# When the splits of the weights are given to the scheduler: at the first unit, or three half chunks ahead

## The chip, the cores and the metric

The kernel runs on one core of one Trainium2 chip. The metric is the device time of one execution in microseconds (us), the median of several runs. Engines: TensorE (PE; its weight loads are PEld), VectorE (DVE), ScalarE (ACT), GpSimd (POOL) and SyncE (SP), which here only issues loads.

## The reference

One decoder layer for 256 tokens of width 2048, in float32. Three token mixers read the same normalised input, their outputs are gated and merged, and a gated MLP follows. Cut to what matters:

```python
h = rmsnorm(x, norm_attn[l])
(q_n, kc_n, ..., q_h, f_h, i_h, g_h, gates) = jnp.split(h @ w_in[l], split_at, axis=-1)
o_nsa = nsa_mixer(...)        # compressed, selected and sliding-window attention
o_sb = stick_breaking(q_s, k_s, v_s)
o_hg = hgrn2(q_h, f_h, i_h, g_h, lb_all[l], hg_norm_gain[l])   # gated linear recurrence
y = jnp.einsum('btnc,ncd->btnd', jnp.stack([o_nsa, o_sb, o_hg], axis=2), w_branch[l])
x = x + jnp.sum(gsig * y, axis=2) @ w_out[l]
x = x + conv_ffn(rmsnorm(x, norm_ffn[l]), w_up[l], conv_w[l], conv_b[l], w_down[l])
```

Some 313 MB, nearly all of it weights, go through the load queue, each weight once for 256 tokens.

## The kernel before

The weights stream in as **chunks** of 128x2048 float32 (1 MB, a tile `raw`, three buffers), loaded on SP's queue. Each chunk is worked on as two **halves** of 128x1024. A half has to be **split** before TensorE can use it: ScalarE rounds it to a high part `whi` (a CAST, L291) and VectorE subtracts to get the low part `wlo` (L292). `whi` and `wlo` have three buffers each, so the split of half h can start when TensorE is done with half h-3. A half feeds 16 or 12 matmuls. There are 593 halves, numbered here from 0 in the order of their use.

The work is a list of **units** (`plan`), in order: first recurrence group, second recurrence group, two stick-breaking groups, gates and branch products, the sparse-attention projections, more gates and branch products, the output projection, the MLP up (44 units) and down. `run` takes units from the list; `unit_b`, `unit_b2`, `unit_a` and `unit_g` call `half` (or `split_to`) for each half they need. The token mixers' own work (`hgrn`, `stick`, `nsa_keys`, `nsa`) is written as generators; after each half `pump` lets the first generator write its next piece, so mixer work stands between the units' matmuls.

A scheduler then sets each engine's order. Of the instructions that it reckons ready, it takes the one that was written first; each engine runs its list strictly in that order. So the place in which a split is *written* decides whether it goes ahead of mixer work that is ready at the same time.

`split_to(n)` (L82) writes splits until n halves are done, and `half` (L127) calls it with the present half plus 1 and then plus `ahead` = 3. In `split_to` the name `n` is also set inside the loop, to the width of a piece:

```python
while self.nsplit < min(n, 2 * len(self.src)):
    ...
    n = 1024 if self.nsplit else 512
```

So after the first pass the loop's bound is 512 and then 1024, beyond the number of halves: the first call writes the loads and the splits of all weights, ahead of everything that the units and mixers write later.

Lines that the prediction names: L184/L185 and L227 to L229 are the units' matmuls, with high and low parts. L234/L235 add up the two sums of a finished `unit_b` (ScalarE, VectorE); L780 (GpSimd) or L782 (VectorE) then scales the result. L436/L437 end `hgrn`; L318 is a scan in the second group's `hgrn`. L502/L503, L504 (Ln) and L508 (Exp) are in `rstd_feat`, and with L517 and L523 they make `norm_feat`, which normalises four query tiles of the sparse attention; L649 makes 16 matmuls of scores from them. L805 is a sigmoid on the gates. Ln, Exp and sigmoid each have an ACT_TABLE_LOAD ahead of them where ScalarE's function changes. `keep_warm` (L210) writes 11 matmuls at the start that only keep TensorE busy.

Of the kernel before, what the change touches and what calls it, by code (L numbers as in the profile page):

```python
# [45 lines left out]
class Net:  # L46
# [35 lines left out]
    def split_to(self, n):  # L82

        nc = self.nc
        while self.nsplit < min(n, 2 * len(self.src)):
            i, j = divmod(self.nsplit, 2)
            self.load_to(i + 1)
            if self.src[i].shape[1] < 2048:
                if not j:
                    self.parts[self.nsplit] = self.split_gate(self.raw[i])  # L90
                self.nsplit += 1
                continue
            raw = self.raw[i][:, 1024 * j:1024 * (j + 1)]
            hi = self.wp.tile([P, 1024], F32R, name="whi", bufs=3)
            lo = self.wp.tile([P, 1024], F32R, name="wlo", bufs=3)
            n = 1024 if self.nsplit else 512
            for c in range(0, 1024, n):
                self.splits.append(self.parts_of(raw[:, c:c + n], hi[:, c:c + n], lo[:, c:c + n]))
                self.casts.append(self.cast)
            self.parts[self.nsplit] = (hi, lo)  # L100
            self.nsplit += 1
# [1038 lines left out]
```

## Time and profile before

| | us |
|---|---|
| median of 3 runs | 1755.03 |
| the runs | 1753.78 to 1756.65 |
| the profiled execution | 1755.64 |
| its span, first to last instruction | 1753.9 |
| TensorE busy | 1744.5 (99%) |
| VectorE busy | 1111.6 (63%) |
| ScalarE busy | 949.4 (54%) |
| GpSimd busy | 127.4 (7%) |

A busy time is the union of an engine's instructions; matmuls overlap, so two that follow each other at 0.23 us each show 0.39 us of length. An instruction's start is therefore the safer mark than its end. Mixer stages run from the start to about 900 us, the MLP from about 1036 us on.

### The profile page before, as it was taken

How to read it: one execution, taken by the hardware profiler on the slowest of the kernel's cores; microseconds unless marked ns; L12 is line 12 of the kernel's file. 1: busy time of each engine (PE TensorE's matmuls, PEld its weight loads, DVE VectorE, ACT ScalarE, POOL GpSimd, SP SyncE). 2: the span in 40 equal slices, each digit the busy share in tenths (PEclk: the TensorE clock that was granted, in tenths of full speed). 3: DMA queues.
4: the chain of work that ended last, by engine and by line, in shares of the span. 5: the costliest groups of instructions: out<-in, count | busy, mean ns of one | idle time of the engine just before them, and what ended most of it. 6: DMA issues, size and time to landing. Idle time of an engine off the chain costs nothing.

```text
span 1753.9 us, 22831 instructions
## 1 busy us (share of the span) xinstructions
PE 1744.5 (99%) x9095; PEld 1487.4 (85%) x9095; DVE 1111.6 (63%) x1421; ACT 949.4 (54%) x1236; POOL 127.4 (7%) x114
## 2 busy tenths in 40 slices
PE   9999999999999999999999999999999999999999
PEld 7888888888888888888888888888888888888887
DVE  6588686756457555765566567777777777644443
ACT  7464745665445575555544565555555555533332
POOL 1110000000001000100011001111111001000000
PEclk9999999999999999999999999999999999999999
DMA  7544443545556444444456555555555555555663
GB/s 285 188 176 162 148 169 144 193 167 179 195 189 253 161 181 168 168 163 152 165 177 231 192 177 187 192 190 192 192 192 192 189 186 188 192 202 200 209 206 109
DMA packets 47835, 324.53 MB, mean 185 GB/s; under 512 B 5440, under 2 KB 5952, under 8 KB 9968
## 3 DMA queue, kind: packets, MB, share of 16 engines
q1 hardware_dynamic: 44784, 313.47, 50.3%
q0 software_dynamic: 1792, 7.50, 1.1%
q10 hardware_dynamic: 1152, 2.10, 0.3%
q8 instruction: 71, 1.16, 0.3%
q14 instruction: 36, 0.29, 0.0%
HBM read 320.96 MB, written 2.10 MB: 184 GB/s over the span
## 4 chain that ended last, share of the span: by engine, by line
PE 98%; ACT 1%; DVE 1%; DMA 0%; issue 0%; SPq 0%; DVEq 0%
PE acc L184 30%; PE acc L185 16%; PE acc L227 11%; PE acc L229 11%; PE acc L228 11%; PE mx L227 5%; PE mx L229 5%; PE mx L228 5%; PE mx L410 1%; PE mx L712 1%; PE mx L680 1%; PE mx L594 0%; DMA raw<-wb_in 0%; PE mx L831 0%; ACT whi L291 0%; PE mx L700 0%
## 5 line engine op out<-in xcount | busy, mean ns | idle before, releaser
L292 DVE TENSOR_TENSOR wlo<-raw,whi 128x1024 fp32r<-128x1024 f32 (+1 forms) x593 | 744.1, 1255 | 528.3 <-ACT whi L291 527.2
L291 ACT CAST whi<-raw 128x1024 fp32r<-128x1024 f32 (+1 forms) x594 | 622.3, 1048 | 667.4 <-PE acc L229 274.1
L184 PE MATMUL acc<-xs,whi 128*128 128x512 f32 x2304 | 808.2, 394 | 1.9 <-ACT whi L291 1.9
L185 PE MATMUL acc<-xs,wlo 128*128 128x256 f32 x2304 | 649.3, 282 | 1.3 <-DVE wlo L292 1.3
L184 PEld LDWEIGHTS acc<-xs,whi 128*128 128x128 f32 x2304 | 433.1, 188 | 97.7 <-ACT whi L291 3.1
L185 PEld LDWEIGHTS acc<-xs,wlo 128*128 128x128 f32 x2304 | 436.2, 189 | 3.7 <-DVE wlo L292 2.8
L227 PE MATMUL acc<-whi,xs 128*128 128x512 f32 x672 | 266.2, 396 | 0.1
L229 PE MATMUL acc<-whi,xs 128*128 128x512 f32 x672 | 262.0, 390 | 0.0
L228 PE MATMUL acc<-wlo,xs 128*128 128x512 f32 x672 | 261.6, 389 | 0.0
L229 PEld LDWEIGHTS acc<-whi,xs 128*128 128x128 f32 x672 | 126.1, 188 | 27.1
L227 PEld LDWEIGHTS acc<-whi,xs 128*128 128x128 f32 x672 | 126.3, 188 | 25.3 <-issue 0.2
L228 PEld LDWEIGHTS acc<-wlo,xs 128*128 128x128 f32 x672 | 126.3, 188 | 25.0 <-issue 0.2
L228 PE MATMUL mx<-wlo,act 128*128 128x512 f32 x352 | 136.9, 389 | 0.0
L227 PE MATMUL mx<-whi,act 128*128 128x512 f32 x352 | 136.9, 389 | 0.0
L229 PE MATMUL mx<-whi,act 128*128 128x512 f32 x352 | 136.9, 389 | 0.0
L1028 POOL TENSOR_TENSOR u<-u,rb 128x512 f32<-128x512 f32 x44 | 52.5, 1192 | 524.0 <-DVE u L235 524.0
L229 PEld LDWEIGHTS mx<-whi,act 128*128 128x128 f32 x352 | 66.1, 188 | 13.8
L228 PEld LDWEIGHTS mx<-wlo,act 128*128 128x128 f32 x352 | 66.1, 188 | 13.7
L227 PEld LDWEIGHTS mx<-whi,act 128*128 128x128 f32 x352 | 66.1, 188 | 13.6
L780 POOL TENSOR_TENSOR b<-b,rb 128x512 f32<-128x512 f32 x24 | 36.7, 1532 | 543.7 <-DVE b L235 489.6
L227 PE MATMUL acc<-whi,bo 128*128 128x512 f32 x192 | 75.7, 394 | 0.0
L229 PE MATMUL acc<-whi,bo 128*128 128x512 f32 x192 | 74.9, 390 | 0.0
(251 smaller groups left out, 1247.9 us busy)
## 6 DMA issues: line engine op xcount, KB each, us to landing
raw<-wb_up SPq DMA_DIRECT2D x88, 1024.0 KB, 4.8
raw<-wa_in SPq DMA_DIRECT2D x68, 1024.0 KB, 4.8
raw<-wb_in SPq DMA_DIRECT2D x53, 1024.0 KB, 4.8
raw<-wa_dn SPq DMA_DIRECT2D x44, 1024.0 KB, 4.8
raw<-wa_br SPq DMA_DIRECT2D x24, 1024.0 KB, 4.8
raw<-wa_out SPq DMA_DIRECT2D x16, 1024.0 KB, 4.8
b<-cw POOLq DMA_DIRECT2D x8, 512.0 KB, 4.8
raw<-wb_in SPq DMA_DIRECT2D x5, 512.0 KB, 9.2
```

Of the source, the lines that this page charges most:

```text
L184: mm(ps[:, j], hi[:, n], x(kt, slice(0, 2), al), start=kt == 0, stop=False)
L185: self.tail = mm(ps[:, j, T:], lo[:, n], x(kt, 0, al), start=False, stop=kt == KT - 1)
L227: mm(ps[tt], x(kt, 0, s), hi[:, k], start=kt == 0, stop=False)
L228: mm(ps[tt], x(kt, 0, s), lo[:, k], start=False, stop=False)
L229: mm(ps[tt], x(kt, 1, s), hi[:, k], start=False, stop=kt == 4 * n - 1)
L291: self.cast = self.nc.scalar.copy(hi, x)
L292: return self.nc.vector.tensor_tensor(lo, x, hi.bitcast(F32), op=ALU.subtract)
L410: mm(ps[:, h, blk], ke[:, 2 * pr + h, t], qe[:, 2 * pr + h, t], start=True, stop=True)
L680: mm(ps, q[g][:, hl, tt * P:(tt + 1) * P], kk[:, g::2, :w], start=True, stop=True)
L712: mm(po[h][:, tq], vv[:, kb, (2 * u + g) * P:(2 * u + g + 1) * P], pT[:, i], start=False, stop=i == n - 1)
L780: net.scaled(lambda: nc.gpsimd.tensor_tensor(d, d, rb2, op=ALU.mult))
L1028: nc.gpsimd.tensor_tensor(u[:, :, 2:], u[:, :, 2:], rb2, op=ALU.mult)
```

## The change

The width of a piece gets a name of its own, so the loop's bound stays the argument. The splits (and the loads with them) are then written by each call only as far as it asks: three halves ahead of the half in use. No instruction is added or taken away.

```diff
@@ split_to
-            n = 1024 if self.nsplit else 512
-            for c in range(0, 1024, n):
-                self.splits.append(self.parts_of(raw[:, c:c + n], hi[:, c:c + n], lo[:, c:c + n]))
+            w = 1024 if self.nsplit else 512
+            for c in range(0, 1024, w):
+                self.splits.append(self.parts_of(raw[:, c:c + w], hi[:, c:c + w], lo[:, c:c + w]))
```

What moves is the order on TensorE, VectorE and ScalarE. GpSimd's and SP's lists stay as they were, so no load changes its place. Counted by the number of splits that stand ahead of it, 721 of VectorE's 827 other instructions and 520 of ScalarE's 610 keep their place; most others move by one split, and on TensorE 20 of 546 mixer instructions move. Three places follow.

**The norm of the queries (`norm_feat` in `nsa`), ScalarE, about 647 us.** Before, from the last of three casts of weights on (t_7175 to t_7181 are the four tiles of sums, b_7255 a gate):

```order
L504 ACTIVATE t_7177<-mx,eps 128x512
L291 CAST nh<-t_7179 128x512
L291 CAST whi<-raw 128x1024
L291 CAST nh<-t_7181 128x512
L504 ACTIVATE t_7179<-mx,eps 128x512
L805 ACT_TABLE_LOAD
L805 ACTIVATE b_7255<-acc,rcol 128x512
L291 CAST whi<-raw 128x1024
L504 ACT_TABLE_LOAD
L504 ACTIVATE t_7181<-mx,eps 128x512
L291 CAST whi<-raw 128x1024
L508 ACT_TABLE_LOAD
```

Casts of weights stand between the norm's instructions here. Now, in the same place (t_5253 to t_5259 are the same four tiles):

```order
L291 CAST whi<-raw 128x1024 x3
L504 ACT_TABLE_LOAD
L504 ACTIVATE t_5253<-mx,eps 128x512
L504 ACTIVATE t_5255<-mx,eps 128x512
L291 CAST nh<-t_5257 128x512
L805 ACT_TABLE_LOAD
L805 ACTIVATE b_5347<-acc,rcol 128x512
L504 ACT_TABLE_LOAD
L504 ACTIVATE t_5257<-mx,eps 128x512
L291 CAST nh<-t_5259 128x512
L805 ACT_TABLE_LOAD
L805 ACTIVATE b_5347<-acc,rcol 128x512
```

and directly behind these, on the same engine:

```order
L504 ACT_TABLE_LOAD
L504 ACTIVATE t_5259<-mx,eps 128x512
L508 ACT_TABLE_LOAD
L508 ACTIVATE t_5253<-t_5253 128x512
L508 ACTIVATE t_5255<-t_5255 128x512
L508 ACTIVATE t_5257<-t_5257 128x512
L508 ACTIVATE t_5259<-t_5259 128x512
L291 CAST whi<-raw 128x1024 x4
```

Eighteen instructions now stand between two casts of weights (those of halves 210 and 211) where at most four stood.

**The scores, TensorE, same place.** Before, the first seven of the 16 score matmuls stand behind half 212 and the other nine five to seven halves later; now all stand around the first matmul of half 211:

```order
L502 MATMUL mx<-nh,onesr 128x512
L227 MATMUL acc<-whi,bo 128x512
L228 MATMUL acc<-wlo,bo 128x512
L503 MATMUL mx<-nh,onesr 128x512
L229 MATMUL acc<-whi,bo 128x512
L649 MATMUL mx<-kcmp,b_4771 128x15 x4
L649 MATMUL mx<-kcmp,b_5008 128x15 x2
L227 MATMUL acc<-whi,bo 128x512
L649 MATMUL mx<-kcmp,b_5008 128x15 x2
L649 MATMUL mx<-kcmp,b_4771 128x15 x4
L649 MATMUL mx<-kcmp,b_5008 128x15 x4
L228 MATMUL acc<-wlo,bo 128x512
```

They moved ahead by 23 to 107 of the units' matmuls, and L503 with them stands nearer to half 211.

**The end of the first `hgrn`, VectorE, about 196 us**, while the second group's last unit runs. Before (t_4227 and t_4256 are the two results):

```order
L436 TENSOR_TENSOR t_4227<-t_4227,b_3608 128x512
L437 SCALAR_TENSOR_TENSOR t_4227<-mx,sc,t_4227 128x512
L292 TENSOR_TENSOR wlo<-raw,whi 128x1024
L235 TENSOR_TENSOR b_4324<-acc,b_4324 128x512
L292 TENSOR_TENSOR bo<-t_4227,bo 128x2x256
L292 TENSOR_TENSOR wlo<-raw,whi 128x1024
```

and now (t_1552, t_1587):

```order
L436 TENSOR_TENSOR t_1552<-t_1552,b_793 128x512
L436 TENSOR_TENSOR t_1587<-t_1587,b_793 128x512
L235 TENSOR_TENSOR b_1669<-acc,b_1669 128x512
L437 SCALAR_TENSOR_TENSOR t_1552<-mx,sc,t_1552 128x512
L292 TENSOR_TENSOR wlo<-raw,whi 128x1024
L292 TENSOR_TENSOR bo<-t_1552,bo 128x2x256
```

The low part of half 62 has moved behind the second L436 and behind L235. At the end of the second `hgrn` (half 94) the same stands, with L782 ahead of the low part as well.

## Rows read from the trace of the kernel before

**Rows 1.** The page, part 2: granted TensorE clock in 40 slices.

```profile
PEclk9999999999999999999999999999999999999999
```

**Rows 2.** Waits of TensorE: engine, line, releaser: us in total, times, longest us.

```profile
PE acc L184 <- ACT whi L291: 1.9, 2, 1.0
PE acc L185 <- DVE wlo L292: 1.3, 3, 0.6
PE mx L649 <- DVE b L523: 0.9, 1, 0.9
```

**Rows 3.** Windows: stretch, busy us of five engines (x), granted clock, DMA share, GB/s.

```profile
10.00:12.00 2.00, 0.98 (x4) 0.30 (x2) 1.08 (x2) 1.59 (x3) 0.00 (x0) 1.00 1.00 412
12.00:14.00 2.00, 1.47 (x6) 1.31 (x6) 2.00 (x5) 2.00 (x4) 0.00 (x0) 0.69 1.03 420
14.00:16.00 2.00, 2.00 (x8) 1.65 (x7) 1.95 (x3) 1.88 (x4) 0.00 (x0) 0.50 1.04 426
16.00:18.00 2.00, 2.00 (x13) 1.78 (x12) 2.00 (x6) 2.00 (x5) 0.00 (x0) 0.96 1.03 406
```

**Rows 4.** Timeline of ScalarE at the norm: start, us, instruction, idle before and releaser.

```profile
647.38 1.05 ACT L291 CAST whi<-raw 128x1024 fp32r<-128x1024 f32 x1 [1.66 <-PE acc L229]
648.44 1.28 ACT L504 ACT_TABLE_LOAD   x1
649.74 1.27 ACT L504 ACTIVATE t<-mx,eps 128x512 f32<-128x512 f32 x2
650.89 0.62 ACT L291 CAST nh<-t 128x512 fp32r<-128x512 f32 x1
651.41 1.05 ACT L291 CAST whi<-raw 128x1024 fp32r<-128x1024 f32 x1
654.88 0.69 ACT L805 ACTIVATE b<-acc,rcol 128x512 f32<-128x512 f32 x1
660.76 1.15 ACT L508 ACTIVATE t<-t 128x512 f32<-128x512 f32 x2
```

**Rows 5.** Timeline of TensorE at the norm.

```profile
657.49 0.39 PE L227 MATMUL acc<-whi,bo 128*128 128x512 f32 x1
662.93 0.96 PE L649 MATMUL mx<-kcmp,b 128*128 128x15 f32 x8
664.83 1.06 PE L649 MATMUL mx<-kcmp,b 128*128 128x15 f32 x6 [0.94 <-DVE b L523]
665.95 0.50 PE L227 MATMUL acc<-whi,xs 128*128 128x512 f32 x1
682.67 0.96 PE L649 MATMUL mx<-kcmp,b 128*128 128x15 f32 x8
```

**Rows 6.** Timeline of VectorE at the norm.

```profile
661.49 1.42 DVE L523 SCALAR_TENSOR_TENSOR b<-b,sc,t 128x512 f32<-128x512 f32 x2 [0.79 <-ACT t L508]
```

**Rows 7.** Timeline of VectorE where the first recurrence group ends.

```profile
197.41 1.21 DVE L292 TENSOR_TENSOR wlo<-raw,whi 128x1024 fp32r<-128x1024 f32 x1
198.54 0.68 DVE L235 TENSOR_TENSOR b<-acc,b 128x512 f32<-128x512 f32 x1
199.74 2.32 DVE L292 TENSOR_TENSOR wlo<-raw,whi 128x1024 fp32r<-128x1024 f32 x1
214.68 1.26 DVE L318 TENSOR_TENSOR_SCAN b<-rst,b 128x256 f32<-128x256 f32 x2
```

**Rows 8.** Timeline of GpSimd, same place.

```profile
199.30 1.68 POOL L780 TENSOR_TENSOR b<-b,rb 128x512 f32<-128x512 f32 x1 [41.69 <-DVE b L235]
```

**Rows 9.** Timeline of TensorE, same place.

```profile
199.90 0.28 PE L185 MATMUL acc<-xs,wlo 128*128 128x256 f32 x1
214.81 0.39 PE L185 MATMUL acc<-xs,wlo 128*128 128x256 f32 x1 [0.62 <-DVE wlo L292]
```

**Rows 10.** Timeline of VectorE where the second recurrence group ends.

```profile
302.97 1.21 DVE L292 TENSOR_TENSOR wlo<-raw,whi 128x1024 fp32r<-128x1024 f32 x1
```

**Rows 11.** Timeline of TensorE, same place.

```profile
305.47 0.28 PE L185 MATMUL acc<-xs,wlo 128*128 128x256 f32 x1
```

## The prediction

> **What bounds the kernel now.** I read the page first. TensorE is busy for 99% of the span, and its granted clock reads 9 in all 40 slices [rows 1]. The view of waits comes next: TensorE's matmuls waited 1.9 us for high parts, 1.3 us for low parts and 0.9 us for the norm ahead of the scores [rows 2]. That is 4.1 us in all, and some of it is the start. So TensorE is the bound, and the splits arrive in time almost everywhere. A change of order on ScalarE or VectorE has hardly anything to win: were every one of these waits to go, the time would be 1755.0 - 4.1 = 1750.9. It can lose wherever a split comes so late that TensorE stands.
>
> What matters is therefore the slack of each half: from the end of its cast, or of its low part, to the first matmul that reads it. In the timelines most halves have 3 to 6 us of it. I laid the new order over this half by half: the rows of ScalarE and VectorE that now stand ahead of a split, at their durations in the trace, against the slack of that split. Moves by one split cost 0.5 to 2.7 us against more slack than that, and go nowhere. In three places the slack is too short. No load moves, SP's and GpSimd's lists being unchanged, so DMA carries no term.
>
> **First place: half 62, about 200 us.** Before, the low part of this half ends at 197.41 + 1.21 = 198.62 [rows 7], and the matmul that reads it starts at 199.90 [rows 9]: slack 1.28. Now a second L436 and the L235 go ahead of it. Both are of L235's size, 0.68 long; L235 and one more of that size fill 198.54 to 199.74 [rows 7], so 0.6 each: 1.2. And L235 starts GpSimd's L780, which in the trace began at 199.30 and ran 1.68 [rows 8]; the low part beside it took 2.32 in place of 1.21 [rows 7]. That overlap falls on half 62's low part now, 1.1 more. 1.2 + 1.1 - 1.28 = **1.0**. Behind it, half 67 waits already [rows 9]. It gets one more scan ahead of it, 1.26 / 2 = 0.63 [rows 7], but TensorE arrives 1.0 later, and the half after it gets that scan's time back, so I add nothing. Bounds: 0, if the overlap falls elsewhere, to 1.9, if the later casts come late too.
>
> **Second place: half 94, about 305 us.** The low part ends at 302.97 + 1.21 = 304.18 [rows 10], its reader starts at 305.47 [rows 11]: slack 1.29. L436, L235 and L782 now go ahead, all of L235's size, 0.6 each from start to start as above: 1.8. GpSimd has no part in this. 1.8 - 1.3 = **0.5** (0.2 to 0.8).
>
> **Third place: the norm, half 211.** The cast of half 210 ends at 648.44 in the trace [rows 4]. Now 18 instructions of ScalarE follow before the cast of half 211. Six are table loads, each 1.30 to the start of the next (648.44 to 649.74): 7.8. Four are Ln, 0.58 each (two fill 649.74 to 650.89): 2.3. Two casts of nh, 0.52 each (650.89 to 651.41): 1.0. Two sigmoids of 0.69, 0.6 net: 1.2. Four Exp, two in 1.15: 2.2. Sum 14.5, so the string ends at 663.0 and half 211's cast at 664.0, where before it began at 651.41 [rows 4]. Everything that the string itself waits for, the norm's sums from TensorE and the finished gates, is there in time, since TensorE runs ahead.
>
> TensorE has work until 657.49, when half 211 began before [rows 5]. Then it stands, first in the scores: they need all four L523 of VectorE, which follow the Exp at 0.71 each (1.42 for two [rows 6]) and end at about 664.3. The last ten scores are 20 passes at 0.12 (eight passes take 0.96 [rows 5]): 2.4. So half 211's second matmul starts at 664.3 + 2.4 = 666.7, in place of 657.7: 9.0 later. Part of that comes back. In the trace TensorE spent 662.93 to 665.95 on seven scores and the wait between them [rows 5], 3.0, and 18 passes of the other nine, some of them at 682.67 [rows 5], 2.2. Both are done by then now. 9.0 - 3.0 - 2.2 = **3.8**. Bounds: 2.5, if the string closes up by a tenth, to 5.5, if ScalarE waits within it.
>
> **The clock after that wait.** [...] One stretch like the start's costs 1.7. If the score matmuls do not lift the clock, their 2.4 us run twice as long, and the streams behind them may lose up to two stretches: 5.8. From below, 0: the 0.94 us wait at 664.83 [rows 5] was followed by no fall. I take 1.7 and a part of the scores, **2.6**, nearest to the start's row. [...]
>
> **The sum.** 1.0 + 0.5 + 3.8 + 2.6 = 7.9. The profiled execution took 1755.64, its span 1753.9, 0.6 above the median; so I expect a span of about 1761.8, and 1755.03 + 7.9 = 1762.9, or 1763, as the median.
>
> **Rivals.**
> *The clock stays up.* The scores may be enough activity, or the fall may come before the wait ends and be over. Then 1.0 + 0.5 + 3.8: 1760.3. For it: no fall in the whole trace after the start. Against it: no wait of that length is in it.
> *The clock falls for longer.* All of the 5.8, and a further 1.7 at half 67, where TensorE then waits 1 us or more: 1755.0 + 5.3 + 5.8 + 1.7 = 1767.8 at most, 1766.1 without half 67.
> *A table load holds ScalarE for twice its row.* Six times 1.28 more, 7.7, all of it in TensorE's wait: 1770.6. Against it: in the trace the Ln starts 1.30 after its load's start [rows 4]. [...]
> *The other side: not slower.* The string is covered. The scores' 32 passes and their wait move into it, 5.2 us that before cost TensorE time. If the later loads of the string cost nothing, because a table is kept, it is 5 x 1.30 = 6.5 shorter; half 211 is 2.5 late, and the place gains 2.7. With the 1.5 of the first two: 1753.8, no change that can be told. It decides at a string of about 9 us. Against it: the Ln's load shows its 1.28 [rows 4], though Ln had been in use earlier in the kernel.
>
> A measurement of this kernel tells about 0.2%, 3.5 us, from no change.
>
> **How the numbers follow.** Forecast (1761.5 to 1765) 0.50; clock stays up 0.22; clock falls for longer 0.16; double loads 0.02; covered 0.07; faster by a wait's removal that I do not see 0.03. The first four are slower by over 0.2%: 0.90. Covered is the same: 0.07. Faster: 0.03. The range reaches from the clock that stays up, with the first place at its lower bound (1759), to the long fall (1767.8), which leaves out the last three cases and the ends of the bounds.
>
> **What would show it.** In the trace after: between two casts of weights at about 650 us, 18 instructions and 14 to 15 us of ScalarE; TensorE's L649 waiting for L523 some 5 us, in one or two pieces; a granted clock of 0.50 for 3 us or more behind it; the 0.9 us wait ahead of L649 at 664 gone; a wait of about 1 us of L185 for the low part at 200 us and of half of that at 305 us; nothing new from 700 us on, where only the up and down matmuls keep their rows. I am wrong if L649's wait is below 2 us, if TensorE waits somewhere else for over 1 us, or if the clock stays at 1.00.

## The result and the profile after

The changed kernel took 1763.93 us (median of 6 runs, 1763.29 to 1764.95), the kernel before 1754.66 in the runs beside it: 9.3 us more, a ratio of 1.0052 (95% interval 1.0039 to 1.0065). The profiled span went from 1753.9 to 1763.2, by the same 9.3.

The waits of TensorE after (engine, line, releaser: us in total, times, longest us) answer to [rows 2]:

```profile
PE mx L649 <- DVE b L523: 5.2, 1, 5.2
PE acc L185 <- DVE wlo L292: 2.8, 6, 1.0
PE acc L184 <- ACT whi L291: 1.6, 3, 0.8
```

One new wait stands above all others, at the scores of the norm. The windows around it (stretch, busy us of five engines, granted clock, DMA share, GB/s) show what came with it:

```profile
650.00:661.00 11.00, 7.40 (x32) 5.42 (x30) 1.39 (x2) 10.88 (x13) 0.00 (x0) 1.00 0.29 95
661.00:674.65 13.65, 12.01 (x44) 10.95 (x45) 7.36 (x10) 5.11 (x8) 0.00 (x0) 0.50 0.21 78
674.65:690.00 15.35, 15.35 (x69) 12.65 (x69) 10.88 (x14) 6.62 (x7) 3.52 (x2) 1.00 0.45 145
```

For 13.65 us the granted clock is 0.50, and TensorE works for 12.0 of them. The kernel before had no such place here: the slices of [rows 1] are too wide to tell, but the clock in its trace has one fall alone, that of [rows 3], from 12.76 to 16.17 us. The cause of the wait is the string on ScalarE, which answers to [rows 4]:

```profile
647.16 1.05 ACT L291 CAST whi<-raw 128x1024 fp32r<-128x1024 f32 x1 [1.66 <-PE acc L229]
648.23 1.28 ACT L504 ACT_TABLE_LOAD   x1
649.52 1.26 ACT L504 ACTIVATE t<-mx,eps 128x512 f32<-128x512 f32 x2
650.67 0.62 ACT L291 CAST nh<-t 128x512 fp32r<-128x512 f32 x1
651.31 1.28 ACT L805 ACT_TABLE_LOAD   x1
652.61 0.69 ACT L805 ACTIVATE b<-acc,rcol 128x512 f32<-128x512 f32 x1
...
661.10 2.19 ACT L508 ACTIVATE t<-t 128x512 f32<-128x512 f32 x4
663.20 2.92 ACT L291 CAST whi<-raw 128x1024 fp32r<-128x1024 f32 x3
```

Between the cast of half 210 and that of half 211, 18 instructions took 648.23 to 663.20, 15.0 us, without a pause. VectorE's four L523 follow the Exp, answering to [rows 6]:

```profile
661.83 2.74 DVE L523 SCALAR_TENSOR_TENSOR b<-b,sc,t 128x512 f32<-128x512 f32 x4 [5.32 <-ACT t L508]
```

TensorE, answering to [rows 5]:

```profile
657.01 0.39 PE L229 MATMUL acc<-whi,bo 128*128 128x512 f32 x1
662.64 2.74 PE L649 MATMUL mx<-kcmp,b 128*128 128x15 f32 x12 [5.24 <-DVE b L523]
665.22 0.77 PE L227 MATMUL acc<-whi,bo 128*128 128x512 f32 x1
665.79 4.28 PE L649 MATMUL mx<-kcmp,b 128*128 128x15 f32 x20
669.91 0.77 PE L228 MATMUL acc<-wlo,bo 128*128 128x512 f32 x1
...
674.33 0.55 PE L229 MATMUL acc<-whi,bo 128*128 128x512 f32 x1
674.71 0.40 PE L227 MATMUL acc<-whi,bo 128*128 128x512 f32 x1
```

It could have gone on at 657.24 (a matmul starts every 0.23) and went on at 662.64: 5.4 us. In the kernel before the scores lost 1.4 here (14 passes of 0.115 in the 3.0 us of [rows 5]), so the wait costs 4.0 more. Each of the 16 score matmuls is two passes. The 32 passes took 2.58 + 4.12 = 6.7 us where 32 at the 0.12 of [rows 5] take 3.84, and twelve streams (unit matmuls of 512 columns) took 0.57 + 4.80 in place of 12 x 0.23: 2.9 + 2.6 = 5.5 us for the lower clock.

The two recurrence groups, VectorE, GpSimd and TensorE, answer to [rows 7 to 11]:

```profile
197.59 1.88 DVE L292 TENSOR_TENSOR wlo<-raw,whi 128x1024 fp32r<-128x1024 f32 x1
197.09 1.29 POOL L780 TENSOR_TENSOR b<-b,rb 128x512 f32<-128x512 f32 x1 [41.46 <-DVE b L235]
199.52 0.39 PE L185 MATMUL acc<-xs,wlo 128*128 128x256 f32 x1 [0.36 <-DVE wlo L292]
214.91 0.39 PE L185 MATMUL acc<-xs,wlo 128*128 128x256 f32 x1 [0.99 <-DVE wlo L292]
305.15 0.39 PE L185 MATMUL acc<-xs,wlo 128*128 128x256 f32 x1 [0.30 <-DVE wlo L292]
```

Laying each matmul's start in the one trace over the start of the same matmul in the other gives the whole 9.3:

| stretch | later by, ahead of it | behind it | cost | forecast |
|---|---|---|---|---|
| start to 195 us | 0 | -0.9 | -0.9 | 0 |
| half 62, 200 us | -0.9 | -0.3 | +0.6 | 1.0 |
| half 67, 213 to 218 us | -0.3 | -0.35 | -0.05 | 0 |
| 218 to 245 us, no wait | -0.35 | -0.75 | -0.4 | 0 |
| half 94, 305 us | -0.75 | -0.2 | +0.55 | 0.5 |
| the norm, 650 to 715 us | -0.2 | +9.3 | +9.5 | 3.8 + 2.6 |
| 715 us to the end | +9.3 | +9.3 | 0 | 0 |

### The profile page after: what moved, and what is told of

Read it like the earlier page. It is cut to its first block, busy times and chain, and to the rows that moved or that the text cites. A ratio compares the mean times of both kernels' runs of the same rounds, so it can differ in the third digit from the quotient of the medians.

```text
span 1763.2 us, 22826 instructions
## 1 busy us (share of the span) xinstructions
PE 1748.4 (99%) x9095; PEld 1490.7 (85%) x9095; DVE 1109.2 (63%) x1421; ACT 948.3 (54%) x1236; POOL 128.3 (7%) x114
## 4 chain that ended last, share of the span: by engine, by line
PE 97%; ACT 2%; DVE 1%; DMA 1%; SPq 0%; issue 0%; DVEq 0%
PE acc L184 29%; PE acc L185 15%; PE acc L227 11%; PE acc L229 11%; PE acc L228 11%; PE mx L228 5%; PE mx L227 5%; PE mx L229 5%; PE mx L410 1%; PE mx L712 1%; PE mx L680 1%; DMA b<-xT 1%; PE mx L594 0%; PE mx L831 0%; PE mx L649 0%; ACT L504 0%
## 5 line engine op out<-in xcount | busy, mean ns | idle before, releaser
L184 PE MATMUL acc<-xs,whi 128*128 128x512 f32 x2304 | 806.5, 393 | 1.6 <-ACT whi L291 1.6
L185 PE MATMUL acc<-xs,wlo 128*128 128x256 f32 x2304 | 648.6, 282 | 2.8 <-DVE wlo L292 2.8
L184 PEld LDWEIGHTS acc<-xs,whi 128*128 128x128 f32 x2304 | 432.1, 188 | 96.7 <-ACT whi L291 3.0
L185 PEld LDWEIGHTS acc<-xs,wlo 128*128 128x128 f32 x2304 | 435.3, 189 | 6.0 <-DVE wlo L292 5.3
L227 PE MATMUL acc<-whi,bo 128*128 128x512 f32 x192 | 76.8, 400 | 0.0
L780 POOL TENSOR_TENSOR b<-b,rb 128x512 f32<-128x512 f32 x24 | 36.9, 1540 | 540.6 <-DVE b L235 476.2
L228 PE MATMUL acc<-wlo,bo 128*128 128x512 f32 x192 | 75.9, 395 | 0.0
```

What stands on the lines that cost most here:

```text
L184: mm(ps[:, j], hi[:, n], x(kt, slice(0, 2), al), start=kt == 0, stop=False)
L185: self.tail = mm(ps[:, j, T:], lo[:, n], x(kt, 0, al), start=False, stop=kt == KT - 1)
L227: mm(ps[tt], x(kt, 0, s), hi[:, k], start=kt == 0, stop=False)
L228: mm(ps[tt], x(kt, 0, s), lo[:, k], start=False, stop=False)
L780: net.scaled(lambda: nc.gpsimd.tensor_tensor(d, d, rb2, op=ALU.mult))
```

## The experiments

The theory read from the trace: the norm is all of the loss, 4.0 us of it the wait and 5.5 the clock, and the clock fell because TensorE stood. The runs of before beside the first four kernels had a median of 1755.54, beside the next four 1755.39, beside the last three 1755.34; ratios are against those. Every run also has its mean granted clock on record, to 0.001. A run at 1.000 (as rounded) lost less than 1 us to the lower clock; each 0.001 below that stands for about 1.8 us of a span of 1755, an estimate from the span's length that the two traces bear out: before, with 3.41 us at 0.50, has 0.999, and the change, with 13.65, 0.996.

### The norm put back, and the norm alone

```
 def split_to(self, n):          (norm_undone)
+    if self.nuse >= 150:
+        n = 2 * len(self.src)
 def split_to(self, n):          (norm_only)
+    n = max(n, 210)
```

> The change up to half 150 (about 440 us), and from there on the order of before: all further splits are written at once, so the norm at 648 us has its casts between its pieces again. Theory (the norm alone costs 9.5 us, made of 3.9 of wait and 5.65 at the half clock; half 62 and half 94 cost 0.1 and 0.6; the start, without its fall of the clock, gives 0.9 back): 1754.7 + 0.7 - 0.9 = 1754.5 (1753.5 to 1755.5), L649 waiting 0.9 us as before and no granted clock of 0.50 near 660 us. Rival (the splits' lower rank costs a little all along, the norm being only where it shows): at least a third of the 9.3 stays, 1757.8 or more. For the start: if the order sets it, the granted clock stays 1.00 at 12 to 16 us as in the changed kernel; if the landing of the first loads sets it, either may be seen.

> The reverse: all splits up to half 209 are written at the first unit, as before, and from there on only as far ahead as asked for, as in the change. Start, half 62 and half 94 stand as before, the norm and all behind it as in the change. Theory: 1754.7 + 9.5 = 1764.2 (1763.2 to 1765.2), L649 waiting for L523 5.2 us, the granted clock 0.50 for about 13.7 us from 661 us on. Rival (the loss is spread): 1759 to 1761. For the start: a fall of the clock at 12.8 us if the order sets it, and then 1764.2; without the fall, which the landing of the loads would explain, about 1763.3.

norm_undone: 1756.04 us, ratio 1.0004 (0.9995 to 1.0013). norm_only: 1763.25, ratio 1.0045 (1.0033 to 1.0058), with L649 waiting 5.3 us and a clock of 0.50 for 13.65 us. So the loss is at the norm, and its rival, a loss spread along the kernel, falls: with the norm put back nothing can be told from the kernel before. The sizes were not met as well: norm_only is 7.7 over its runs of before where 9.5 was expected (its span 8.7 over that of before), and norm_undone 0.5 over where -0.2 was. The windows of norm_undone show something that bears on both:

```profile
660.00:664.63 4.63, 3.64 (x23) 3.13 (x21) 4.29 (x6) 4.60 (x7) 0.00 (x0) 1.00 0.32 88
664.63:668.04 3.41, 3.34 (x9) 2.60 (x10) 2.46 (x3) 1.05 (x2) 3.08 (x2) 0.50 0.64 267
```

Here the order is that of before, with the same wait of 0.9 us for L523, and still the clock fell for 3.4 us, which it did not in the trace of before. So the old order has slower runs too, and the distance of norm_only to their median is smaller. The clocks on record show it: of the 15 runs of before beside these, the two at 1.000 took 1753.7 in the mean, the eleven at 0.999 1755.4 and the two at 0.998 1756.4, while norm_only was at 0.995 or 0.996 in all five. To the two at 1.000 its median is 9.5 over. Where in the kernel the clock fell in a run that has no profile is not on record.

### TensorE kept at work in the wait

```
+with self.tc.issue_after(self.norm_ln.ins):
+    wm = self.mx()
+    for _ in range(22):
+        mm(wm, self.ones_r, self.warm, start=True, stop=True)
 pc = self.mx()...
```

(norm_ln is the norm's last Ln, warm the first tile of x.)

> The change, with 22 matmuls of 512 columns that nobody reads (the ones by the first tile of x) ahead of the first score, where TensorE stands from 657.2 to 662.6: 22 x 0.227 = 5.0 us, inside the wait. The string of ScalarE and the wait for it stay. Theory (3.9 us of the loss is the wait and 5.65 is the lower clock, and a TensorE kept at work does not fall): granted clock 1.00 through the whole place, 32 score passes at 0.11 in place of 0.21, time 1763.9 - 5.65 = 1758.3 (1757.3 to 1759.3). Rival (the clock falls for another reason than TensorE's standing, or the passes are slow for what they read): 1763.9 again, with 0.50 at 661 us. Rival (the added matmuls come late or hold a bank that the norm wants): over 1764.

1762.19 us, ratio 1.0040 (1.0026 to 1.0054): 6.7 over before, where 3.6 had been expected. TensorE's timeline:

```profile
656.49 5.20 PE L647 MATMUL mx<-xs,onesr 128*128 128x512 f32 x22
661.91 1.94 PE L653 MATMUL mx<-kcmp,b 128*128 128x15 f32 x12 [0.21 <-DVE b L523]
663.70 0.48 PE L227 MATMUL acc<-whi,bo 128*128 128x512 f32 x1
664.02 3.48 PE L653 MATMUL mx<-kcmp,b 128*128 128x15 f32 x20
```

and its windows:

```profile
662.00:664.90 2.90, 2.81 (x22) 2.59 (x22) 2.90 (x5) 2.90 (x5) 0.00 (x0) 1.00 0.02 6
664.90:671.72 6.82, 6.82 (x23) 5.88 (x23) 3.57 (x6) 0.49 (x1) 0.00 (x0) 0.50 0.42 154
```

With the wait filled, the fall came 3.9 us later and lasted half as long, but it came, in the middle of the scores, with TensorE busy for 2.81 of the 2.90 us ahead of it. My theory of the clock was too simple: standing went ahead of the fall in the change, and a run of short passes seems to be another way to it.

### The streams ahead of the scores

```
-mm(pc[:, tt, h], ...)
+with self.tc.issue_after(self.atail.ins):
+    mm(pc[:, tt, h], ...)
```

(atail is the last matmul that unit_a has written.) The second kernel has 32 unread matmuls in the wait as well.

> The change, with the 16 scores in four groups, each held behind the last matmul written ahead of it, so that the streams of half 211 come first behind the wait and the scores stand some halves later. TensorE now waits for half 211's cast, from 657.2 to about 664.2, 7.0 us, in place of 5.4 for L523 (and before lost 1.5 us here). Theory (the scores, 15 columns a pass, do not lift the clock, so in the change their 6.7 us came on top; 4.7 us of the streams behind them did lift it): 0.50 from 661.0 to about 669, loss 7.0 - 1.5 + 2.2, so 1754.4 + 7.7 = 1762.1 (1761 to 1763). Rival (the fall lasts as long as the wait that caused it makes it, whatever runs behind): 0.50 for 13.7 us or more again, 10.4 us of streams at half: 1754.4 + 5.5 + 4.9 = 1764.8. Rival (one stretch of 3.4 us as at the start of the kernel before): 0.50 to 664.4 only, 1759.9.

> The run with the scores behind, plus 32 unread matmuls of 512 columns where TensorE stood there (26 ahead of half 211's first matmul, 5 between it and the next, 1 later): 31 x 0.227 = 7.0 of the 8.3 us of waiting. The string of ScalarE is as in the change. Theory (the clock falls where TensorE stands or where it runs the scores, 15 columns a pass, in one piece; neither is left): granted clock 1.00 from the start to the end, 13 streams that took 0.43 each take 0.23 again, 2.8 us less than that run: 7.9 - 2.8 = 5.1 over the kernel before, 1759.8 at its 1754.7 or 1760.6 beside runs of 1755.5 (+-1). Rival (the unread matmuls do not count for the clock, as the run with 22 of them in the wait might also be read): 0.50 at about 660 to 670 us again and no gain.

scores_behind: 1763.55 us, ratio 1.0046 (1.0034 to 1.0059), 8.0 over before (7.4 expected). Its windows, and in the second fence those of warm_spread:

```profile
656.80:660.40 3.60, 0.40 (x2) 0.00 (x0) 0.00 (x0) 3.54 (x5) 0.00 (x0) 1.00 0.00 0
660.40:664.10 3.70, 0.00 (x1) 0.00 (x1) 2.45 (x4) 3.69 (x7) 0.00 (x0) 0.50 0.00 0
664.10:670.64 6.54, 5.85 (x13) 4.28 (x14) 3.70 (x4) 1.84 (x2) 0.00 (x0) 0.50 0.44 158
```

```profile
660.40:664.10 3.70, 2.77 (x13) 1.97 (x12) 2.79 (x5) 3.69 (x7) 0.00 (x0) 1.00 0.00 0
664.10:670.64 6.54, 6.54 (x30) 5.21 (x29) 4.58 (x4) 2.56 (x3) 0.00 (x0) 1.00 0.49 162
```

With streams right behind the wait the clock came back 6.5 us after TensorE went on, in place of 12.0 in the change (662.64 to 674.65), although the wait was longer (6.9 us for the cast and 0.7 for the low part). So in these two runs what ran behind the wait went with how long the fall lasted, and the scores did not lift the clock (0.50 through all 32 passes of the change). The rival of a fall that is as long whatever runs falls by this profile, and by the clocks of the five runs, 0.997 and 0.998 where the change has 0.996 in all six. warm_spread: 1761.65, ratio 1.0038 (1.0026 to 1.0051), 6.3 over before (5.1 expected, 1.2 too few), with a mean clock of 1.000 in the profile and 1.00 from 640 to 690 us (three of the five runs at 1.000, two at 0.999): without the long wait and without the passes in one piece no fall is left here, and unread matmuls do count (scores_behind, without them, had 0.50 for 10.2 us). Both together take the clock's part away, and the wait's part stays.

### The passes alone, in the kernel before

```
+at = self.atail                (8 yields ahead, in place of 6)
 for tt in range(2):
     for h in range(HEADS):
-        mm(pc[:, tt, h], ...)
-        if h % 4 == 3:
-            yield
+        with self.tc.issue_after(at.ins):
+            mm(pc[:, tt, h], ...)
+...                             (four yields behind the piece)
```

> The kernel before with nothing changed but the place of the 16 scores: all 32 passes in one piece, two to three halves later than before, with streams of 512 columns on both sides and nothing to wait for. The 1.5 us that before waited for L523 go. Theory (the short passes alone let the clock fall): a stretch of 0.50 that begins in them or just behind, 3.4 us or more; the time is 1.5 less and 1.6 to 3 more than before, a ratio of 1.000 to 1.001. Rival (only standing lowers it): 1.00 there, and 1.5 us less than before, a ratio of 0.999. At the start the old order: a fall of the clock at 8 to 13 us if the order sets that, none if chance does.

1759.78 us, ratio 1.0024 (1.0015 to 1.0033), where 1.000 to 1.001 was expected, with two falls of the clock. The second is the one looked for, in TensorE's timeline:

```profile
684.05 0.39 PE L229 MATMUL acc<-whi,xs 128*128 128x512 f32 x1
684.27 3.64 PE L651 MATMUL mx<-kcmp,b 128*128 128x15 f32 x32
687.76 0.51 PE L227 MATMUL acc<-whi,xs 128*128 128x512 f32 x1
```

```profile
684.00:688.08 4.08, 4.08 (x35) 3.96 (x35) 0.20 (x2) 2.33 (x2) 0.00 (x0) 1.00 0.70 253
688.08:691.49 3.41, 3.41 (x10) 2.64 (x9) 2.87 (x6) 0.41 (x1) 0.00 (x0) 0.50 0.01 5
```

The passes run at full clock for 3.5 us with no wait on either side, and right behind them 0.50 is granted for 3.4 us. So the short passes in one piece do it alone, here once. They need not in every run: of the 11 runs one had a clock of 1.000 and took 1755.14 us, near the median of before, and one had 0.999 and took 1756.74. The first fall (664.19 to 671.01) stands behind a wait that I had not seen coming:

```profile
PE acc L227 <- ACT b L807: 2.9, 1, 2.9
```

The next unit's bank is free only when the second sigmoid of the gates has read it, and that sigmoid stands at the end of the string (L807 here, L805 in the other listings). In the kernel before, the scores and their own wait filled these 3 us, so the 0.9 us of [rows 2] could not be won by moving the scores: the bank was late next.

### The rank of the splits by one half chunk more

```
-self.split_to(i + ahead)
+self.split_to(i + max(ahead, 4))
```

> The change with one number altered, the splits written four half chunks ahead in place of three. At the norm one cast, half 211's, now stands in the middle of the string, so TensorE has its 24 matmuls (12 by 0.45 = 2.7 us) to do while ScalarE goes on; the last Exp ends at about 660.5 and the scores, all 32 passes in one piece, come right behind half 211. Behind them VectorE takes L655 to L657 (1.2 us) ahead of half 212's low part. Theory (wait by the rows, clock by short passes and standing): TensorE waits 0.5 to 1 us for L523 and about 2 for half 212's low part, 1.0 to 1.5 more than before there, and the clock falls, 2 to 4 us: 3 to 5.5 over before, about half of the change's loss. Rival (only a wait of 5 us or more lowers the clock): no 0.50, 1 to 1.5 over before less 0.9 of the start: no change. Rival (the distance does not matter, any order of this kind costs the same): 9 over before.

1758.32 us, ratio 1.0017 (1.0008 to 1.0026): 2.9 over before, where 3 to 5.5 was expected. No wait at 200 or 305 us is left, L649 waits nowhere above 0.2 us, and the norm shows the two parts again, smaller (waits, windows):

```profile
PE acc L228 <- DVE wlo L292: 1.8, 1, 1.8
```

```profile
664.55:671.38 6.83, 5.06 (x12) 3.84 (x12) 4.53 (x6) 2.28 (x3) 0.00 (x0) 0.50 0.52 202
```

Against three half chunks (9.3) and all of them (0), one more takes two thirds of the loss away.

### The scores spread, with the old order

The changed order up to half 20 only, and the scores behind as in scores_behind.

> Made of what the runs so far point to: the change up to half 20 alone (about 50 us), all further splits written at once as before, and the scores in four groups, each held behind the last matmul written ahead of it. Half 62, half 94 and the norm's splits stand as in the kernel before. Theory: the 1.5 us of waiting for L523 at the norm go, and no fall of the clock there, since no four groups of passes stand together; at the start no fall of the clock, if the order sets that, 0.9 less. In all 1.5 to 2.4 less than before, a ratio of 0.9986 to 0.9992. Rival (what stands behind the scores, L655 on, comes late for the next stage or runs into the splits): a new wait near 680 us and no gain. Rival (the start is chance): 1.5 less or none told from before.

1756.88 us, ratio 1.0011 (1.0002 to 1.0020): slower, not faster. TensorE waits 2.9 us for the sigmoid's bank, as in one_piece, and the clock falls for 3.4 us behind it. Neither of the rivals was this wait.

### The gates' sigmoids behind the norm's last Ln

```
 for tt in range(2):
-    nc.scalar.activation(t[:, tt], ps[tt], AF.Sigmoid, ...)
+    with tc.issue_after(net.norm_ln.ins):
+        nc.scalar.activation(t[:, tt], ps[tt], AF.Sigmoid, ...)
```

Put into the change (gates_after), into the kernel before (gates_after_before), and into norm_only (gates_after_210).

> The change, with the sigmoids of the gates (L805) held behind the last Ln written so far, and nothing else. At the norm the two sigmoids now stand behind the four Exp in place of between the Ln: three table loads in place of six, and the casts of halves 211 and 212 fall between the norm's pieces. The scores stand in four groups, two to four halves later. Theory (the six loads, 7.8 of the string's 15.0 us, made the wait, and the wait with the scores in one piece made the clock fall): the string with its two casts ends at about 661.1 (648.2 + 1.3 + 1.15 + 0.5 + 1.05 + 0.5 + 0.6 + 1.05 + 0.6 + 1.3 + 2.2 + 1.3 + 1.2), half 211's matmuls start in time, TensorE waits nowhere near the norm, no 0.50 there; of the loss only half 62 and half 94 stay (0.6), and the 1.5 us of waiting that before had here go: a ratio of 0.9990 to 1.0000. Rival (any split order by distance is late here, the loads are not the cause): a wait of 3 us or more and at least 4 us over before, a ratio of 1.0023 or more.

> The kernel before with the same one edit: the gates' sigmoids behind the last Ln. Its splits stay first in rank. String: 14.7 us with four casts of weights in it, to about 663.2; the next stream's bank is free some 0.5 us late, where in the kernel before the scores and the wait for L523 took 3.0 us in the same place. Theory (the two sigmoids between the Ln, not the splits' rank, set what the norm costs in either kernel): 1.0 us less than before at the norm and no stretch of 0.50 there, a ratio of 0.9985 to 0.9997. Rival (the bank's wait, 2.9 us in the two runs where the scores were moved off it, is the sigmoid's own place in the string and comes here as well): 1.4 more than before, 1.0005 to 1.0015.

> The first run of these three with all splits up to half 209 written at the first unit, as before: halves 62 and 94 stand as in the kernel before, the norm as in that run. Theory: 0.6 less than it, 1.5 less than before, a ratio of 0.9985 to 0.9995, the best of all. Rival (the two places cost nothing in the end, since half 67's wait gives it back): the same as that run.

gates_after: 1756.20 us, ratio 1.0005 (0.9996 to 1.0014). ScalarE's string in it:

```profile
649.48 1.28 ACT L504 ACT_TABLE_LOAD   x1
...
657.39 1.28 ACT L508 ACT_TABLE_LOAD   x1
658.68 2.20 ACT L508 ACTIVATE t<-t 128x512 f32<-128x512 f32 x4
660.90 1.28 ACT L806 ACT_TABLE_LOAD   x1
662.19 1.27 ACT L806 ACTIVATE b<-acc,rcol 128x512 f32<-128x512 f32 x2
663.35 1.04 ACT L291 CAST whi<-raw 128x1024 fp32r<-128x1024 f32 x1
```

Three loads in place of six, two casts of weights between the pieces, and the 9.5 us of the norm are gone: TensorE waits 0.3 and 0.8 us there, at 664, and the clock stays at 1.00. The ratio is still above the 0.9990 to 1.0000 expected: the 1.5 us that before waited here did not go, and halves 62 and 94 still cost 0.6 and 0.55. At an equal clock the kernel is slower than before: its five runs at 1.000 took 1755.96 to 1756.20, the seven of before at 1.000 1753.33 to 1754.76. The splits' rank alone does not make the loss, nor the loads alone; it takes a rank by which the splits yield and a string that alternates between tables. This profile differs from the change at the start, too, where the order is the same:

```profile
7.96:14.79 6.83, 6.34 (x19) 4.73 (x20) 3.93 (x8) 4.76 (x9) 0.00 (x0) 0.50 1.02 413
```

gates_after_before: 1754.20, ratio 0.9994 (0.9985 to 1.0002); gates_after_210: 1754.31, ratio 0.9995 (0.9986 to 1.0004). In the first the bank's wait is 1.3 us where 0.5 was expected and before lost 1.4, so the gain expected did not come as a gain at this place. Both lie below 1 and neither can be told from the kernel before: no version here beats it for certain. Seven of the 11 runs of gates_after_before were at a clock of 1.000 and took 1753.9 in the mean, as the seven of 27 of before did; what differs is how many runs fall, and why was not tested.

The starts of the matmuls, laid over those of before in each run's profile as in the table above, give what the norm (640 us to the end) cost in it, wait and clock together:

| kernel | us at the norm | us at 0.50 there |
|---|---|---|
| the change | 9.5 | 13.65 |
| norm_only | 9.55 | 13.65 |
| scores_behind | 9.2 | 10.2 |
| warm_wait | 7.5 | 6.8 |
| warm_spread | 7.1 | 0 |
| one_piece | 6.0 | 6.8 + 3.4 |
| ahead_4 | 3.8 | 6.8 |
| spread | 3.15 | 3.4 |
| norm_undone | 1.5 | 3.4 |
| gates_after, gates_after_before, gates_after_210 | 0.0 | 0 |

So norm_only holds the whole of the norm's loss, as expected, and norm_undone, whose orders and waits there are those of before, shows what one fall of 3.4 us costs: 1.5.

## Why the prediction was right, and where by luck

The time was forecast as 1763 and measured as 1763.9, the span as 1761.8 and 1763.2. By its steps:

**The bound.** TensorE was the bound, nothing could be won, and no load took part: right. From 715 us on nothing changed.

**Half 62** (1.0 forecast, 0.6 there). The step that failed is the overlap with GpSimd's L780, put at 1.1. It ran from 197.09 to 198.38, so only the first part of the low part's 197.59 to 199.47 lay beside it, and this took 1.88 in place of 1.21: 0.67, not 1.1. With that, 1.2 + 0.67 - 1.28 = 0.6, as measured. That half 67 "adds nothing" was right: one wait of 1.0 stands where two (0.6 and 0.2) stood before, and the steps between matmuls around them are as long in sum. The 0.4 that came back from 218 to 245 us has no wait in it and was in no step: two matmuls that follow each other there (L184, L185) took 0.347 us in place of 0.353. Between 44 and 56 us the trace after has 0.347 too and gates_after, with the same order, 0.353; so this pace belongs to the run at least in part, and its cause stays open.

**Half 94** (0.5): 0.55.

**The norm's string and the wait** (3.8): right, in each link. String 14.5 forecast, 15.0 measured, 18 instructions with six loads; the wait for L523 in one piece. At full clock half 211's second matmul would have started at 662.64 + 3.84 + 0.23 = 666.7, as forecast, or at 664.57 + 2.4 = 667.0 if the last L523 had held up the last ten scores; the give-back of 5.2 came too. Net 4.0, or 4.3 by the second count with 5.2 left for the clock.

**The clock** (2.6, bounds 0 to 5.8): it fell, as forecast, 1.6 us before the wait ended, but cost 5.5. The step that failed is "I take 1.7 and a part of the scores". Its 1.7 is the start's: in [rows 3] the clocks of 0.69, 0.50 and 0.96 from 12 to 18 us come to 1.2 + 2.0 + 0.2 = 3.4 us at half the clock, 1.7 lost. That one such stretch would follow the long wait was the author's estimate; the trace of before shows no fall in mid-kernel, and the change showed 13.65 us at 0.50 there. The upper bound's own two conditions held both: the scores did not lift the clock, all 32 passes ran at half (2.9), and the streams behind them lost 2.6 more. What the step lacked is that the passes are no mere victims: scores_behind shows the clock back 5.5 us sooner without them, and one_piece shows 0.50 for 3.4 us right behind them with no wait on either side. The fall at 661.0 came in a place where TensorE had stood since 657.4; the second of one_piece, at 688.08 with TensorE busy for 4.08 of the 4.08 us ahead of it, is not that case.

**The start** (0): 0.9 less, in no step. The orders of before and after are the same up to about 31 us, where VectorE's first L235 ends. In the trace after, the clock did not fall there, as it did in [rows 3]; in gates_after, with the changed order, it fell for 6.8 us. 0.5 of the 0.9 is there at 30 us and so belongs to the run and not to the change: in the profiles of norm_undone and gates_after, with the same changed order at the start, TensorE was 2.25 us earlier there than in the trace of before, and not earlier at all (0.02 later). 0.1 comes at a wait at 36 us, where the orders differ, and the last 0.3 up to 57 us by the pace named above. How much of this is in the medians is not told by one profile each.

So the sum came out by errors of both signs: +2.9 for the clock and +0.2 for the string's wait, -0.4 for half 62, -0.4 for the pace behind half 67, -0.9 for the start, together 1.4, the distance of the two spans. That the forecast came so near is in part luck: the norm as a whole was forecast at 6.4 and cost 9.5.

**The rivals.** A clock that stays up: refuted. A clock that falls for longer: it did, at the norm, and alone would have given 1766. A load that holds ScalarE for twice its row: the load at 648.23 is followed by the Ln at 649.52, 1.29 later, and so on through the string; refuted. A string that is covered: not in this order, but gates_after is that rival made real. The condition was named as "a string of about 9 us"; what did it there was three loads fewer and two casts of weights inside the string.

**What the runs leave open.** norm_undone and before have the same rows at the norm and one of them shows a fall of the clock; which of the two happens in a given run is not explained here. And one_piece shows its second fall in a single profile, and its runs show that the falls can fail to come.

## What to carry to other kernels

When the rank of ready work is loosened, look for the longest string on an engine that the bound engine needs often, and count its table loads: here 7.8 of 15 us were loads, because two sigmoids fell between the Ln, and one constraint on them undid the norm's loss without touching the rank. A wait of the bound engine cost its own length here and then, where it was long, the lower clock on what followed (in the change 4.0 us net for a wait of 5.2, and 5.5 for the clock); price the second part by the work behind it, and take short passes in one piece at the upper bound (in one_piece 32 of them with no wait were followed by 0.50 for 3.4 us). And before moving work out of a wait, ask what else is late there: the scores covered 2.9 us of waiting for a bank that no row of before showed.

## What was not expected of the hardware

- 32 passes of 15 columns in one piece, TensorE busy for 4.08 of 4.08 us, were followed by 3.4 us of granted clock 0.50 (one_piece, 688.08 to 691.49).
- Near the norm the lower clock lasted 3.4 us (norm_undone, spread), 6.8 (warm_wait, ahead_4), 10.2 (scores_behind) and 13.65 (the change, norm_only).
- At the start, with one order, the clock fell for 6.8 us in one profile (gates_after) and not at all in another (the change). At the norm, with the same order and the same wait of 0.9 us, it fell for 3.4 us in norm_undone and not in the kernel before.
- One kernel's runs spread with the clock: 1753.33 us at a mean of 1.000 to 1758.24 at 0.997 (the kernel before).
